# Recurrence emitted ahead of the other mixers, memory attention second with output tiles of its own, output projection from their tiles on

## The chip, the cores and the metric

One core of one Trainium2 chip runs the whole program, two transformer networks one behind the other. The metric is device microseconds of one execution, lower is better. Engine names are those of the profile: PE is TensorE (matmul), PEld its weight loads, DVE is VectorE, ACT ScalarE, POOL GpSimd, and SP the engine whose queue issues the large loads.

## The reference

Only the first network's front is touched, for 256 tokens of width 1024. Its three mixers read one normalised input `h`, and one projection joins them:

```python
h = rms_norm(x, attn_norm[l])
proj = h @ w_in[l]
q_da, k_da, v_da, rw_cols, q_mem = jnp.split(proj, [c1, c2, c3, c4], axis=-1)
o_da = diff_attention(q_da, k_da, v_da, positions, ...)        # 4 heads, 512 columns
o_rw = rwkv7_time_mix(rw_cols, ...)                            # 4 heads, 256 columns
mem_n = rms_norm(mem, mem_norm[l])
o_mem = memory_attention(q_mem, mem_n, w_mem_kv[l], ...)       # 4 heads, 256 columns
mixed = jnp.concatenate([o_da, o_rw, o_mem], axis=-1)
x = x + mixed @ w_out[l]
x = x + hierarchical_moe(rms_norm(x, ffn_norm[l]), ...)        # 16 experts
```

`diff_attention` takes two softmax maps per head and subtracts one from the other; `rwkv7_time_mix` is a recurrence over the tokens (state 64x64 per head). Everything behind the mixture of experts, four feed-forward layers and two more mixers, is the second network.

## The kernel before

The program is written as calls on tiles; a scheduler then sets each engine's order. It works through the emitted order and lets later work fill where it thinks that an engine would wait, so the emitted order is a priority. Once built, each engine's queue is fixed.

Weights come as 128x4096 fp32 tiles (2 MB) into a ring of three buffers named `raw` (`load`, L85 to L92; the issues are on SP). `split` (L94 to L101) makes of 1024 columns a rounded high part `wh` on ACT (L99) and the rest `wl` on DVE (L100), in a ring of three pairs here. Every projection takes three products per tile, high by high, low by high, high by low (`mm3`, L105 to L107, called "products" below); a projection of 512 columns over 1024 has 48 of them, in two PSUM banks.

`mixers` (L551 to L625) holds the change. The recurrence is a Python generator: `rwkv_inputs` (L644) projects its 1024 columns, and `rwkv` (L667) is emitted in pieces at each `next(rwkv)`. Between the pieces stand the attention's k projection (into `lent`), its q projection, the memory's transposes `memT` and key/value projection `mkv`, the head norms and transposes (`heads_T`), the memory's queries (`win_m`) and the v projection `dv`. Then come `diff_attn` (L1013), the last piece of the recurrence (its result is `Y`), `mem_attn` (L1064), the transposes of `Y` (L606), and the output projection.

- Vector stage of the recurrence: L698 to L746 make `kr`, `nb` and `kt` on DVE and ACT, with small PE steps at L705, L726, L750 and L758. The first products that need `nb` are at L777. L794 is the helper of the chain of 64x64 products behind it.
- Difference attention, per head and map: scores (L295, L296), added bias and row minimum on DVE (L301), exponential on ACT (L303), reciprocal (L309), scaling and subtraction (L1023 to L1026). Then transposes (L1033), the copy `pT` (L1035) and the products with `dv` (L1039 to L1041), which gather in two PSUM banks `po` until all four heads are done. At the end each half is copied (`do`, L1046), squared, summed (L1051), given its root on POOL (L112), scaled (L1053), transposed (L1056), scaled (L1058) and split into `oh` (L1061) and `ol` (L1062).
- Memory attention: scores L1076, minimum L1077, exponential L1080, scaling L1084, transposes L1095, copy L1098, products L1101.
- `project_back` (L345): eight k tiles of the mixed row (0 to 3 attention, 4 and 5 recurrence, 6 and 7 memory). It takes all but the last `tail` tiles for both token halves, then the tail half by half; half 0 gathers in two `acc` banks, half 1 in two `rk` banks.

PSUM has three `acc`, two `tr` and three `rk` banks. Behind the mixers, `logits` (L1108) and the routing at the head of `moe` (L1135) end in the first expert product, L1303. The experts' weights are loaded into buffers that fall free earlier: halves of 1 MB (L1267), the recurrence's scratch among them, `wh` and `wl` pairs (L1263) and `raw` tiles.

## Time and profile before

| what | us |
|---|---|
| median of 3 runs | 1427.64 (1427.21 to 1431.28) |
| the profiled execution's own time | 1430.63 |
| its span | 1428.9 |
| front: start of the trace to the end of the output projection | 188.0 |
| from there to the first expert product | 17.6 |

A trace row gives start, duration and, in brackets, the idle time before it with the instruction that ended it. PE's durations overlap, because matmuls are pipelined; the spacing of their starts tells what one costs. The fp32 score, transpose and small products may have several records per instruction. PEclk is the granted TensorE clock as a share of 2.4 GHz, so 0.50 is its level of 1.2 GHz. In the order listings below, names carry numbers that tell buffers apart, and the changed kernel's line numbers are higher (L105 to L107 are L117 to L119, lines further on 9 higher).

### The profile page before, as it was taken

The numbers are of one execution on the slowest core, as the hardware profiler recorded it, in microseconds if no ns is written. First come the engines' busy times: TensorE is split into PE (matmuls) and PEld (weight loads), VectorE is DVE, ScalarE is ACT, GpSimd is POOL, SyncE is SP. The second block draws the span as 40 slices with busy tenths as digits, with TensorE's granted clock in tenths as the row PEclk, the third lists the DMA queues.
The fourth block names the chain that finished last, engine by engine and source line by source line (L and its number), as shares of the span: only waits on it lengthen the run. The fifth ranks groups of instructions, "written<-read, shape, count | busy, mean of one in ns | idle before, by whom it ended". The sixth has DMA issues, their size and how long they took to land.

```text
span 1428.9 us, 18895 instructions
## 1 busy us (share of the span) xinstructions
PE 1378.0 (96%) x7650; PEld 1051.2 (74%) x7650; DVE 747.7 (52%) x1250; ACT 610.0 (43%) x961; POOL 77.5 (5%) x123
## 2 busy tenths in 40 slices
PE   8999989998998999999999999999999989999997
PEld 7787664343336888888777888878888877788886
DVE  6867641121116655457865655455554567555543
ACT  5545421011113544347454544345444366545442
POOL 1133100000000000000110000000000000000001
PEclk9999889999998999999999999999999999999999
DMA  7262489999956555446334555445553642464420
GB/s 315 93 230 91 185 327 414 409 424 428 422 216 236 183 191 184 153 171 251 115 106 147 184 191 183 178 178 188 189 205 125 241 158 75 139 229 177 177 89 30
DMA packets 35370, 293.81 MB, mean 206 GB/s; under 512 B 3728, under 2 KB 8112, under 8 KB 16080
## 3 DMA queue, kind: packets, MB, share of 16 engines
q1 hardware_dynamic: 29952, 286.58, 53.1%
q10 hardware_dynamic: 5328, 5.98, 1.3%
q8 instruction: 62, 1.02, 0.3%
q14 instruction: 28, 0.23, 0.0%
HBM read 291.45 MB, written 1.10 MB: 205 GB/s over the span
## 4 chain that ended last, share of the span: by engine, by line
PE 65%; DVE 3%; ACT 1%; issue 1%; ACTq 0%; POOLq 0%; POOL 0%
PE acc L105 20%; PE acc L107 20%; PE acc L106 20%; PE tr L213 1%; PE acc L329 1%; DVE wl L100 1%; PE tr L325 1%; PE acc L296 1%; PE acc L295 1%; PE acc L330 0%; ACT sq L119 0%; DVE h L376 0%; DVE h L378 0%; DVE xf L139 0%; ACT wh L99 0%
## 5 line engine op out<-in xcount | busy, mean ns | idle before, releaser
L100 DVE TENSOR_TENSOR wl<-raw,wh 128x1024 fp32r<-128x1024 f32 (+1 forms) x349 | 426.1, 1224 | 377.0 <-ACT wh L99 374.9
L99 ACT CAST wh<-raw 128x1024 fp32r<-128x1024 f32 (+1 forms) x349 | 364.6, 1048 | 408.6 <-PE acc L107 358.1
L105 PE MATMUL acc<-wh,xh 128*128 128x512 f32 (+1 forms) x896 | 334.5, 375 | 2.4 <-ACT xh L140 1.8
L107 PE MATMUL acc<-wh,xl 128*128 128x512 f32 (+2 forms) x896 | 333.2, 373 | 1.7 <-DVE xl L141 1.5
L106 PE MATMUL acc<-wl,xh 128*128 128x512 f32 (+1 forms) x896 | 333.1, 372 | 0.0
L105 PEld LDWEIGHTS acc<-wh,xh 128*128 128x128 f32 x896 | 170.4, 190 | 32.2 <-ACT xh L140 3.0
L107 PEld LDWEIGHTS acc<-wh,xl 128*128 128x128 f32 x896 | 170.3, 190 | 31.7 <-DVE xl L141 3.7
L106 PEld LDWEIGHTS acc<-wl,xh 128*128 128x128 f32 x896 | 170.5, 190 | 28.3 <-DVE lent L732 0.6
L107 PE MATMUL acc<-wh,hl 128*128 128x512 f32 x352 | 137.5, 391 | 0.0
L106 PE MATMUL acc<-wl,hh 128*128 128x512 f32 x352 | 137.1, 389 | 0.0
L105 PE MATMUL acc<-wh,hh 128*128 128x512 f32 x352 | 137.0, 389 | 0.0
L106 PEld LDWEIGHTS acc<-wl,hh 128*128 128x128 f32 x352 | 66.1, 188 | 13.8
L105 PEld LDWEIGHTS acc<-wh,hh 128*128 128x128 f32 x352 | 66.1, 188 | 13.5
L107 PEld LDWEIGHTS acc<-wh,hl 128*128 128x128 f32 x352 | 66.1, 188 | 13.4
L105 PE MATMUL acc<-xh,wh 128*128 128x256 f32 x224 | 67.6, 302 | 1.2 <-ACT wh L99 0.6
L106 PE MATMUL acc<-xl,wh 128*128 128x256 f32 x224 | 65.6, 293 | 0.6 <-DVE xl L141 0.6
L107 PE MATMUL acc<-xh,wl 128*128 128x256 f32 x224 | 65.7, 295 | 0.0
L111 POOL TENSOR_SCALAR rstd<-ss 128x1 f32<-128x1 f32 x22 | 9.3, 422 | 965.8 <-ACT sq L119 964.3
L1303 PE MATMUL acc<-half,xe 128*64 128x512 f32 x248 | 59.6, 596 | 0.0
L1336 DVE TENSOR_SCALAR yf<-tr,gate 128x512 f32<-128x512 f32 x16 | 12.0, 751 | 81.0 <-PE tr L1329 80.8
L105 PEld LDWEIGHTS acc<-xh,wh 128*128 128x128 f32 x224 | 45.2, 202 | 5.0 <-issue 2.4
L106 PEld LDWEIGHTS acc<-xl,wh 128*128 128x128 f32 x224 | 45.1, 201 | 1.1 <-DVE xl L141 0.9
(454 smaller groups left out, 1681.5 us busy)
## 6 DMA issues: line engine op xcount, KB each, us to landing
raw<-in_ffn SPq DMA_DIRECT2D x63, 2048.0 KB, 8.0
half<-in_moe SPq DMA_DIRECT2D x45, 1024.0 KB, 12.9
raw<-in_moe SPq DMA_DIRECT2D x13, 2048.0 KB, 16.0
raw<-in_hyb SPq DMA_DIRECT2D x7, 2048.0 KB, 8.2
wl<-in_moe SPq DMA_DIRECT2D x23, 512.0 KB, 13.4
wh<-in_moe SPq DMA_DIRECT2D x23, 512.0 KB, 14.4
raw<-in_win SPq DMA_DIRECT2D x4, 2048.0 KB, 10.7
raw<-in_swa SPq DMA_DIRECT2D x4, 2048.0 KB, 9.2
```

Of the source, the lines that this page charges most:

```text
L99: nc.scalar.copy(hi[:, :n], x)
L100: nc.vector.tensor_tensor(lo[:, :n], x, hi[:, :n].bitcast(F32), OP.subtract)
L105: mm(out, a[0], b[0], start=start, stop=False)
L106: mm(out, a[0], b[1], start=False, stop=False)
L107: mm(out, a[1], b[0], start=False, stop=stop)
L213: nc.tensor.transpose(ps[:, i * 128:(i + 1) * 128], m[:, i * 128:(i + 1) * 128], self.ident)
L295: nc.tensor.matmul(ps[:, 0:128], qT[r, 0:128], kT[r, 0:128], start=True, stop=True)
L296: nc.tensor.matmul(ps[:, 128:384], qT[r, 128:256], kT[r, :], start=True, stop=True)
L325: nc.tensor.transpose(pt[:, i * 128:(i + 1) * 128], s2[e][:, i * 128:(i + 1) * 128], self.ident)
L329: nc.tensor.matmul(po[r, :T], v[0][:, c:c + 64], pT[:, :T], start=True, stop=False)
L1303: last = mm(ps[c][e * 64:e * 64 + 64, :], xe[:, k, o + e * 64:o + e * 64 + 64], w[i][e][:, c * 512:c * 512 + 512], start=k == 0, stop=k == 7)
L1336: nc.vector.tensor_scalar(yf, po[a], gate[:, 0:1], None, OP.mult)
```

## The change

```diff
+class Joined:
+    def __init__(self, a, b):
+        self.a, self.b = a, b
+
+    def __getitem__(self, at):
+        p, k, t = at
+        n = self.a.shape[1]
+        return self.a[p, k, t] if k < n else self.b[p, k - n, t]
...
         parts = {}
-        for b, src in enumerate(wsrc):
-            wd = self.load(src)
-            for i in sorted(range(src.shape[-1] // 1024), key=lambda i: order.index(4 * b + i)):
-                parts[4 * b + i] = self.split(wd[:, i * 1024:(i + 1) * 1024])
+        raw = {}
+        for b in sorted(range(len(wsrc)), key=lambda b: order.index(4 * b)):
+            raw[b] = self.load(wsrc[b])
+            for k in [k for k in order if k not in parts]:
+                if k // 4 not in raw:
+                    break
+                parts[k] = self.split(raw[k // 4][:, k % 4 * 1024:(k % 4 + 1) * 1024])
...
-        rwkv = self.rwkv(self.rwkv_inputs(W, xh, xl, bc))
-        next(rwkv)
+        rw = self.rwkv_inputs(W, xh, xl, bc)
+        mem = [self.sb([D], "mem") for _ in range(2)]
+        for t in range(2):
+            nc.sync.dma_start(mem[t], self.I["mem"][t * 128:(t + 1) * 128])
+        Y = list(self.rwkv(rw))[-1]
         dist, nlam = self.diff_consts()
         k = project(W[3], 512, self.lent("wl"))
-        next(rwkv)
         self.bias_vectors()
-        q = project(W[2], 512, self.lent("wh"))
-        next(rwkv)
-        m = next(self.ring).tile([128, 4096], F32, name="mem", tag="raw")
-        mem = [m[:, :D], m[:, D:2 * D]]
-        for t in range(2):
-            nc.sync.dma_start(mem[t], self.I["mem"][t * 128:(t + 1) * 128])
         m = next(self.ring).tile([128, 4096], F32, name="memT", tag="raw")
...
         mkv = project(self.I["memkv"], 512, [self.sb([512], "mkv") for _ in range(2)], xm)
-        next(rwkv)
         kT = self.heads_T(k, 4, self.col("dak_g"), 1.0, "dkT")
-        qT = self.heads_T(q, 4, self.col("daq_g"), 0.125, "dqT")
-        next(rwkv)
         qm = project(self.I["win_m"], 256, [self.sb([256], "mq") for _ in range(2)])
         mqT = self.heads_T(qm, 2, self.col("memq_g"), 0.125, "mqT")
-        next(rwkv)
         mkT = self.heads_T([z[:, :256] for z in mkv], 2, self.col("memk_g"), 1.0, "mkT")
-        next(rwkv)
+        q = project(W[2], 512, self.lent("wh"))
+        om = [wk.tile([128, 2, T], F32R, name=self.nm("om"), tag=n, bufs=1) for n in ("mh", "ml")]
+        self.mem_attn(mqT, mkT, mkv, *om)
+        qT = self.heads_T(q, 4, self.col("daq_g"), 0.125, "dqT")
         v = project(W[4], 512, [self.sb([512], "dv") for _ in range(2)])
         oh, ol = (self.wk.tile([128, 8, T], F32R, name=self.nm("o"), tag=n, bufs=1) for n in ("xh", "xl"))
         self.diff_attn(qT, kT, v, dist, nlam, oh, ol)
-        Y = list(rwkv)[-1]
         scratch.close()
-        self.mem_attn(mqT, mkT, mkv, oh, ol)
...
+        oh, ol = (Joined(z[:, :6, :], m) for z, m in zip((oh, ol), om))
...
-            nc.scalar.copy(oh[:, 6 + j, :], po[:, :T])
-            nc.vector.tensor_sub(ol[:, 6 + j, :], po[:, :T], oh[:, 6 + j, :].bitcast(F32))
+            nc.scalar.copy(oh[:, j, :], po[:, :T])
+            nc.vector.tensor_sub(ol[:, j, :], po[:, :T], oh[:, j, :].bitcast(F32))
...
-MIX_ORDER = (0, 1, 2, 3, 6, 7, 4, 5)
-TAIL = {"mix": 2, 0: 5, "hyb": 5, 1: 4, 2: 2, "swa": 3, 3: 4}
+MIX_ORDER = (6, 7, 4, 5, 0, 1, 2, 3)
+TAIL = {"mix": 3, 0: 5, "hyb": 5, 1: 4, 2: 2, "swa": 3, 3: 4}
...
-           "a": ((8, 12), (128, 1), (260, 2), (384, 3), (512, 7), (1024, 2))}
+           "a": ((8, 12), (128, 1), (260, 2), (384, 3), (512, 9), (1024, 4))}
```

The whole recurrence now has the highest priority, and all else fills. `mem` lies in buffers of its own and is loaded early; memory attention follows its projections and writes `om`, which `Joined` shows to the output projection as tiles 6 and 7; the q projection comes later, and its weights take the ring buffer that `memT` leaves. Difference attention is last. The output projection loads the second half of its weights first and takes tiles 6, 7, 4, 5 ahead of 0 to 3, with a tail of three.

**First place: PE, the recurrence's vector stage.** In these rows acc_575 and acc_576 are the attention's k projection, tr_494 the transposes of the recurrence's norms. Before:

```order
L107 MATMUL acc_575<-wh_567,xl_97 128x512
L105 MATMUL acc_576<-wh_567,xh_96 128x512
L106 MATMUL acc_576<-wl_568,xh_96 128x512
L107 MATMUL acc_576<-wh_567,xl_97 128x512
L726 MATMUL tr_494<-ident,lent_457 128x128 x4
L105 MATMUL acc_575<-wh_571,xh_96 128x512
L105 MATMUL acc_576<-wh_571,xh_96 128x512
L229 MATMUL tr_840<-bias_const_838 32x384
```

Now (acc_1199 is the k projection, and its first product is the last row):

```order
L759 MATMUL rk_525<-c_94,boN_79_463 128x2 x3
L145 MATMUL tr_1268<-ident,mem_446 128x128 x4
L786 MATMUL rk_545<-kr_464,nb_465 64x128 x2
L786 MATMUL acc_633<-kr_464,kt_466 64x128 x2
L786 MATMUL acc_634<-kr_464,kt_466 64x128 x2
L786 MATMUL acc_633<-kr_464,kt_466 64x128 x2
L786 MATMUL rk_546<-kr_464,nb_465 64x128 x2
L786 MATMUL rk_545<-kr_464,nb_465 64x128 x2
L786 MATMUL rk_546<-kr_464,nb_465 64x128 x2
L814 MATMUL rk_567<-nb_465,kr_464 64x64 x4
L786 MATMUL acc_634<-kr_464,kt_466 64x128 x2
L117 MATMUL acc_1199<-wh_1183,xh_96 128x512
```

All 48 products of the k projection have moved from around and ahead of the vector stage's PE steps to behind the first products that need `nb`.

**Second place: PE, the third and fourth head of the difference attention.** dkT and dqT are its keys and queries, dv its values; NR, Z, S, DW and MT belong to the recurrence. Before:

```order
L903 MATMUL rk_1498<-DW_1438,MT_1437 64x64 x3
L295 MATMUL acc_1697<-dkT_1195,dqT_1222 128x128
L296 MATMUL acc_1697<-dkT_1195,dqT_1222 128x256
L1033 MATMUL tr_1724<-ident,sc_1662 128x128 x3
L903 MATMUL rk_1506<-S_1499,MT_1437 64x64 x4
L915 MATMUL rk_1779<-NR_627,Z_1393 64x64 x4
L915 MATMUL rk_1778<-NR_627,Z_1393 64x64 x4
L295 MATMUL acc_1708<-dkT_1195,dqT_1222 128x128
L296 MATMUL acc_1708<-dkT_1195,dqT_1222 128x256
L1039 MATMUL acc_1652<-dv_1514,pT_1728 128x128
L1040 MATMUL acc_1653<-dv_1514,pT_1728 128x128
```

Now:

```order
L1048 MATMUL acc_1844<-dv_1706,pT_1882 128x128
L1049 MATMUL acc_1845<-dv_1706,pT_1882 128x128
L1050 MATMUL acc_1845<-dv_1707,pT_1882 128x128
L307 MATMUL acc_1889<-dkT_1379,dqT_1679 128x128
L308 MATMUL acc_1889<-dkT_1379,dqT_1679 128x256
L1042 MATMUL tr_1916<-ident,sc_1854 128x128 x3
L307 MATMUL acc_1900<-dkT_1379,dqT_1679 128x128
L308 MATMUL acc_1900<-dkT_1379,dqT_1679 128x256
L1048 MATMUL acc_1844<-dv_1706,pT_1920 128x128
L1049 MATMUL acc_1845<-dv_1706,pT_1920 128x128
L1050 MATMUL acc_1845<-dv_1707,pT_1920 128x128
L117 MATMUL acc_1984<-wh_1990,om_1587 128x512
```

The recurrence's products between the heads are gone. What fills is 12 products of the memory's tiles at the first head's scores, and six at the fourth, of which the last row is the first.

**Third place: PE, the end of the difference attention.** Rows with o are the output projection's, tr_1751 and tr_1943 the transposes of `do`, acc_1890 and its like memory scores. Before:

```order
L1040 MATMUL acc_1653<-dv_1514,pT_1737 128x128
L1041 MATMUL acc_1653<-dv_1515,pT_1737 128x128
L1076 MATMUL acc_1890<-mkT_1414,mqT_1362 128x256 x2
L1076 MATMUL acc_1902<-mkT_1414,mqT_1362 128x256 x2
L1056 MATMUL tr_1751<-ident,do_1742 128x128 x4
L1076 MATMUL acc_1914<-mkT_1414,mqT_1362 128x256 x2
L1056 MATMUL tr_1769<-ident,do_1760 128x128 x4
L1095 MATMUL tr_1927<-ident,ms_1879 128x128 x4
L105 MATMUL rk_1983<-wh_1987,o_1586 128x512
```

Now:

```order
L1050 MATMUL acc_1845<-dv_1707,pT_1929 128x128
L117 MATMUL acc_1985<-wh_1990,om_1587 128x512
L118 MATMUL acc_1985<-wl_1991,om_1587 128x512
L119 MATMUL acc_1985<-wh_1990,om_1588 128x512
L117 MATMUL acc_1985<-wh_1994,om_1587 128x512
L118 MATMUL acc_1985<-wl_1995,om_1587 128x512
L119 MATMUL acc_1985<-wh_1994,om_1588 128x512
L1065 MATMUL tr_1943<-ident,do_1934 128x128 x4
L1065 MATMUL tr_1961<-ident,do_1952 128x128 x4
L614 MATMUL tr_1971<-ident,Y 128x128 x2
L614 MATMUL tr_1976<-ident,Y 128x128 x2
L117 MATMUL acc_1984<-wh_1998,o_1778 128x512
```

The memory's scores have left this place for six products; the transposes of the recurrence's `Y`, and with them the 24 products of tiles 4 and 5, stand behind the transposes of `do`.

## Rows read from the trace of the kernel before

**Rows 1.** The page: its head.

```profile
span 1428.9 us, 18895 instructions
```

**Rows 2.** Windows of the front: each engine's busy us and instructions, granted clock, DMA.

```profile
17.62:39.85 22.23, 22.23 (x187) 21.73 (x185) 14.30 (x22) 15.23 (x26) 1.08 (x8) 1.00 0.66 271
39.85:54.97 15.12, 15.12 (x77) 11.90 (x76) 14.60 (x32) 10.41 (x20) 5.17 (x7) 1.00 0.02 4
54.97:119.14 64.17, 63.06 (x742) 51.86 (x741) 44.80 (x77) 26.26 (x42) 20.18 (x20) 1.00 0.54 199
119.14:147.35 28.21, 27.82 (x437) 22.00 (x436) 21.32 (x90) 17.75 (x60) 6.33 (x7) 1.00 0.11 37
147.35:158.01 10.66, 7.28 (x25) 4.79 (x25) 10.36 (x26) 6.49 (x20) 4.96 (x8) 0.66 0.09 12
158.01:187.99 29.98, 29.98 (x130) 22.40 (x131) 11.58 (x22) 9.69 (x18) 1.46 (x1) 0.95 0.86 351
187.99:205.63 17.64, 13.11 (x76) 12.59 (x74) 12.87 (x45) 5.32 (x10) 1.88 (x4) 0.61 0.86 350
```

**Rows 3.** Timeline of SP, and a window of the start of the experts.

```profile
209.32 0.33 SPq L91 DMA_DIRECT2D raw<-in_moe  x1
...
205.00:210.00 5.00, 5.00 (x24) 1.99 (x23) 0.69 (x1) 0.05 (x1) 0.00 (x0) 0.96 0.01 3
```

**Rows 4.** Timeline of DVE at both ends of the vector stage, and the splits between.

```profile
39.68 0.42 DVE L657 TENSOR_TENSOR cur<-acc,bc 128x256 f32<-128x256 f32 x1 [0.30 <-PE acc L107]
...
54.78 0.40 DVE L738 TENSOR_TENSOR nb<-lent,iw 128x256 f32<-128x256 f32 x1
...
L100 DVE TENSOR_TENSOR wl<-raw,wh 128x1024 fp32r<-128x1024 f32 x5 | 6.1, 1215 | 0.0
```

**Rows 5.** Timeline of PE: two products of the k projection.

```profile
47.68 0.39 PE L106 MATMUL acc<-wl,xh 128*128 128x512 f32 x1
47.91 0.39 PE L107 MATMUL acc<-wh,xl 128*128 128x512 f32 x1
```

**Rows 6.** Timeline of PE: scores of one map, transposes of one head, the start behind.

```profile
137.24 0.49 PE L295 MATMUL acc<-dkT,dqT 64*128 64x128 f32 x2
...
138.09 0.82 PE L1033 MATMUL tr<-ident,sc 128*128 128x128 f32 x3
138.87 0.46 PE L903 MATMUL rk<-S,MT 64*64 64x64 f32 x4
```

**Rows 7.** Timeline of DVE: first and last operations of the fourth head.

```profile
138.92 0.28 DVE L301 CUSTOM_DVE_ANT_0 sc<-acc,dbias 128x128 f32<-128x128 f32 x1
...
143.10 0.74 DVE L1026 SCALAR_TENSOR_TENSOR sc<-sc,den,sc 128x128 f32<-128x128 f32 x2
```

**Rows 8.** Groups of ACT instructions, 119 to 162 us: count, busy us, mean ns, idle.

```profile
L420 ACT ACTIVATE dv<-acc,rstd 128x512 f32<-128x512 f32 x2 | 1.2, 674 | 0.0
L99 ACT CAST wh<-raw 128x1024 fp32r<-128x1024 f32 x1 | 1.0, 1045 | 1.0 <-PE acc L107 1.0
```

**Rows 9.** Timeline of PE behind the attention's last product, which ends at 147.35.

```profile
147.58 2.26 PE L1076 MATMUL acc<-mkT,mqT 64*128 64x256 f32 x8 [0.23 <-ACT do L1046]
152.25 1.12 PE L1056 MATMUL tr<-ident,do 128*128 128x128 f32 x4 [2.41 <-DVE do L1053]
158.01 0.80 PE L105 MATMUL rk<-wh,o 128*128 128x512 f32 x1 [0.74 <-ACT o L1061]
```

**Rows 10.** Windows of 5 us around that wait.

```profile
150.00:155.00 5.00, 2.75 (x8) 1.88 (x8) 4.77 (x13) 2.04 (x8) 3.15 (x5) 0.57 0.01 2
155.00:160.00 5.00, 4.26 (x14) 3.07 (x14) 5.00 (x14) 3.71 (x11) 0.00 (x0) 0.50 0.47 133
160.00:165.00 5.00, 5.00 (x25) 3.60 (x24) 0.80 (x4) 0.58 (x1) 0.00 (x0) 0.90 1.02 429
```

**Rows 11.** Transfers by line, median us from issue to landing.

```profile
raw<-in_memkv SPq DMA_DIRECT2D x1, 2048.0 KB, 7.6
```

## The prediction

> **What bounds the kernel now.** I read the page's head first, for the span of the profiled execution [rows 1], then windows over the front, where each column says how busy an engine is [rows 2]. The reader is to see there that PE is the full engine: 22.23 of 22.23 us, then 15.12 of 15.12, 63.06 of 64.17 and 27.82 of 28.21, the last with DVE at 21.32 and ACT at 17.75 beside it. The recurrence's small products, the projections and the difference attention are interleaved so that something is nearly always ready. Only one place is open: behind the attention's last product, 147.35 to 158.01, PE shows 7.28 of 10.66 and the granted clock is 0.66 of 2.4 GHz.
>
> Second, what follows the front. The experts' buffers are full before the routing is known: between 205 and 210 the DMA engines are at 0.01, and SP issues the next expert load only at 209.32, when a first buffer falls free [rows 3]. No transfer waits to be pulled ahead, so I count a delay of the front as a delay of the end, one for one.
>
> So the question is how much PE time the new order leaves idle between 17.6 us and the first expert product, and how much of the one hole it closes. PE's work is the same in both; the sum below is over idle time and time at half clock.
>
> **A, the recurrence's vector stage.** Between the last input product (39.85) and the first product with `nb`, DVE works from 39.68 until `nb` is written at 54.78 + 0.40 = 55.18 [rows 4], 15.5 us. Five splits lie in it, 1.215 us each, 6.1 in all [rows 4]. PE filled these 15.12 us with the 48 products of the k projection, whose starts are 0.23 apart [rows 5]: 11.0 us, leaving 4.1 for the stage's own small steps. In the new order all 48 stand behind the first products that need `nb`, and an engine's queue is fixed, so they can't fill. The stage itself gets shorter: one split is left ahead of `nb`, so 15.5 - 4 x 1.2 = 10.7, and `nb` comes at 50.4. PE then has 4.1 us to do in 10.5: 6.4 idle. Lower bound 4, if the stage also loses most of the rows that ACT shares with the splits' high parts; upper 10, if the splits only lay in DVE's waits and the stage stays near 15. The splits' rows have no idle time before them, so I stay near the first: **+6**.
>
> **B, the difference attention by itself.** It used to run among the recurrence's last products. Now the recurrence is done, and only 18 memory-tile products are left to lie beside it, 12 at the first head and six at the fourth. Ahead of its first minimum stand two copies `dv` of 0.67 and one cast `wh` of 1.05 on ACT [rows 8], and one split of 1.22 on DVE [rows 4]: 3.6 in all. The chain of one head runs through DVE and ACT; the fourth head took from 138.92 to 143.10 + 0.74 = 143.84 [rows 7], 4.92 us, with six recurrence operations among them. Without them it can lose at best what DVE has idle or elsewhere in it; scaled by DVE's busy share (21.32 of 28.21 [rows 2]) that is 3.7. At half clock its two score pairs cost about 0.6 more, so 5.5 is the upper end. I take 4.5, nearer to the measured head, since most of those operations stood beside a wait. 3.6 + 4 x 4.5 + 1.6 for the last transposes and products gives 23.2. PE's work in it: per head two maps of scores at 0.85 (137.24 to 138.09), the transposes 0.78 (138.09 to 138.87) [rows 6] and about as much, 0.87, for the products with `dv`: 3.35, four times 13.4; and 18 products at 0.23 are 4.1. 23.2 - 17.5 = **+6**, between 2.5 (heads of 3.7) and 10 (heads of 5.5).
>
> The Trainium skill, "Perfetto Trace Analysis", section "Optimization Strategy", says that a kernel with several regimes may gain by interleaving them. The window with PE at 27.82 of 28.21 beside a DVE at 21.32 [rows 2] is such an interleaving, and the change separates what it holds; by that advice B is a loss, by a count of busy time alone it would be nothing. No number above depends on it.
>
> **C, the end of the difference attention.** Before, 10.66 us passed from the last product to the first of the output projection. What PE did in it is worth less: 12 memory scores at 2.26 / 8 = 0.28 each, 3.4, and 12 transposes that took 1.12 for four at half clock [rows 9], so about 1.7 at full, 5.1 together. Lost: 5.6, and some 1.5 more since the first 3 us of products also ran at half clock (0.50 in 155 to 160, 0.90 in 160 to 165 [rows 10]), 7.1 in all. Now the scores are gone from here and six products, 1.4, stand in their place; the transposes of `Y`, with the 24 products of tiles 4 and 5, stand behind the transposes of `do` in PE's queue, so the recurrence's tiles do not cover the wait although they are ready. Two splits of 1.2 stand in DVE's queue in the tail's chain; the memory's minima and the recurrence's last normalisation have left it. I set those against each other, with about 1 us in favour of the shorter queue: 10.66 - 1 - 3.1 + 1.5 = 8.1, so **+1** (from -2, if the chain falls to about 7, to +4, if both splits delay it in full and the clock is half for 24 products).
>
> **D, the second load of the q weights.** The q projection's weights now wait for the ring buffer that `memT` leaves, freed by the last `mkv` product. Its first product comes some 9 us behind that in PE's order, by my count of the products between; a 2 MB load of this kind takes 7.6 us [rows 11], with a split of about 2 us to the first product. **+1** (0 to 3). SP holds nothing behind it that the front needs sooner; the experts' loads there go into buffers that were full in time anyway [rows 3].
>
> **E, the clock behind the stall of A.** The one stall of before was followed by some 3 us of products at half clock, 1.5 lost [rows 10]; A's stall is shorter and has small steps in it: **+1** (0 to 4).
>
> **F, small waits and re-ordered pieces.** The 1.5 us of PE idle between 54.97 and 147.35 (1.11 and 0.39 [rows 2]) may partly go, since now everything fills behind the recurrence: **-1** (-3 to +2). The copies into `om` are those that went into the shared tile before, and `Joined` only chooses between tiles while the program is built: nothing. `mem` now loads early on, beside the first weights (DMA at 0.66 until 39.85 [rows 2]); hidden, since it is needed only behind the whole vector stage, and if it held up the input weights by its size, 1 MB of 2 MB loads of 7.6 us [rows 11], that would be under 4, which the range holds.
>
> **Sum.** 6 + 6 + 1 + 1 + 1 - 1 = +14. It is made against the profiled execution's 1430.63 (span 1428.9 [rows 1]), which stands 3.0 above the median 1427.64; against the median it gives 1427.6 + 14 = **1441.6**.
>
> **The rivals.**
>
> *Contention, not order, set the pace (not slower), 0.13.* Then the engines, once the recurrence has left, run the attention at heads of 3.7: B is 2.5, C falls to -1.5, A stands at its lower bound 4, D and E are nothing, F is -2: +3, 1431, no change that can be measured; with A at nothing as well (the stage short enough to be covered by its own steps) it is slightly faster, 1427 to 1424. For it: DVE's 14.60 busy of 15.12 in the vector stage and 10.36 of 10.66 in the tail [rows 2], so chains there were queues. Against: DVE does 8.5 us of its own between the splits, twice PE's 4.1, so A can't vanish without a faster DVE. It decides if heads come at or below 4.1 us.
>
> *The clock stays at half through the whole attention, 0.17.* PE would do 17.5 us of work in 23, in pieces, behind a stall; half clock (1.2 GHz) there makes heads 5.5 and B 10, E 5, C +4, A, D and F as above: 6 + 10 + 4 + 1 + 5 - 1 = +25, 1453. For it: a window with PE at 2.75 of 5 was granted 0.57, and the next, with 4.26 of 5, still 0.50 [rows 10]. Against: with PE at 27.82 of 28.21 the clock was 1.00, and so far it rose again within 3 us of products. The Trainium skill, "TensorE: Matmul & The Clock Gate", section "HAM oscillation — how this bites in real kernels", puts the cost of being throttled again after waits at half of the throttled time; by it the roughly 10 us at half clock behind the tail of before would have cost 5, while by the rows only the products in them, 1.5, count as lost, since the rest was a wait on DVE and ACT. The trace so far bears the smaller number out, and no run yet shows which holds in the attention.
>
> *The delay is not passed on, or the tiles do cover the tail, 0.06.* If the experts' loads absorbed the shift, or if PE could start on tiles 4 and 5 while the attention ends (24 products, 5.5 us), the total would be 1427 down to 1422. Against the first: full buffers and a DMA share of 0.01 as the experts start [rows 3]. Against the second: the order of the queue, third place above.
>
> **How the numbers follow.** The forecast has 0.64, the rivals 0.13, 0.17 and 0.06. About 0.3% (4.3 us) is what a measurement can tell from no change. Slower than that: the forecast's 0.64, all of the clock rival, less 0.01 for the low ends of the terms falling together, 0.80. Within it: 0.13, most of the first rival, a part of the third and that 0.01. Faster: 0.07, from the first's and third's low ends. The range runs from the first rival's +3 at 1430 to 1455, a little over the clock rival's 1453; below lies about 0.12, above about 0.08.
>
> **What would show it.** PE idle for some 6 us between 40 and 51, where 15.12 of 15.12 stood. PE at about three quarters in the 23 us of the difference attention. A tail of about 10 us between the last product with `dv` and the first of tiles 4 and 5. The output projection ending near 202 where 188.0 stood, the first expert product near 220, and the same distance from there to the end. The forecast is wrong in A if `nb` comes before 46 or k products stand ahead of it; in B if heads come at 4 us or 5.5; and as a whole if the distance from the first expert product to the end changes by more than 3 us.

## The result, and the profile after

| | before | after |
|---|---|---|
| median, us | 1427.43 (1426.86 to 1431.28, 4 runs) | 1445.2 (1443.2 to 1446.9, 4 runs) |
| ratio | | 1.0118, 95% interval 1.0099 to 1.0137 |
| span of the profiled execution | 1428.9 | 1443.0 |
| end of the output projection | 188.0 | 203.9 |
| first expert product | 205.6 | 221.8 |
| from there to the end | 1223.3 | 1221.2 |

Slower, by 17.8 us between the medians and by 14.1 between the two profiled executions; the forecast was +14, 1441.6. That the 14.1 lands on the 14 is closer than a single pair of executions can carry. The delay is complete at the first expert product (+16.1) and nearly all of it reaches the end. Over all the profiled executions below, the stretch behind the first expert product took 1217.5 to 1223.9 us, with no relation to the front; so the time of the first expert product is the finer yardstick for an edit of the front, and each experiment is given with it.

Windows of the kernel after, cut at its own milestones (the answer to [rows 2]; columns as there):

```profile
17.62:39.97 22.35, 22.35 (x181) 21.38 (x179) 14.67 (x23) 15.35 (x26) 2.24 (x11) 1.00 0.66 266
39.97:54.47 14.50, 11.05 (x76) 8.26 (x75) 13.21 (x32) 6.29 (x15) 2.35 (x3) 0.67 0.01 4
54.47:151.25 96.78, 95.77 (x1164) 78.00 (x1162) 62.74 (x129) 44.27 (x90) 28.85 (x30) 1.00 0.37 134
151.25:176.93 25.68, 21.93 (x86) 15.03 (x85) 14.49 (x64) 11.55 (x40) 0.00 (x0) 0.73 0.58 238
176.93:186.83 9.90, 4.62 (x19) 3.25 (x19) 6.75 (x9) 5.05 (x9) 3.71 (x4) 0.72 0.57 205
186.83:203.92 17.09, 17.09 (x74) 14.05 (x73) 6.32 (x9) 3.81 (x5) 0.91 (x1) 0.96 0.91 350
203.92:221.77 17.85, 12.85 (x76) 12.12 (x75) 13.04 (x46) 5.33 (x10) 1.89 (x4) 0.63 0.51 198
```

The rows are: input products; the recurrence's vector stage up to the first product of the k projection; everything up to the end of the v projection; the difference attention up to its last product with `dv`; its tail up to the first output product of tiles 4 and 5; the other output products; routing. The second, fourth and fifth are the three places of the forecast, and each has idle PE time and a granted clock of 0.67 to 0.73. The long row between them is dense (1.01 idle) at full clock, and routing is as long as before (17.64).

What PE waited for between 17 and 222 us (total, times, longest):

```profile
PE tr L1065 <- DVE do L1062: 4.6, 2, 2.9
PE tr L735 <- DVE lent L731: 3.4, 1, 3.4
...
PE tr L1042 <- DVE sc L1035: 2.2, 1, 2.2
PE acc L1048 <- ACT pT L1044: 1.5, 2, 0.9
```

L1065 is the tail, L735 the vector stage, L1042 and L1048 the first and last heads. These are 11.7 us; the same list of before holds 2.4 + 0.7 for its tail. Over the whole stretch from 17.62 to the first expert product PE is idle for 18.5 us where 9.4 stood, and busy for 185.7 where 178.6 stood, with the same products to do. So 9.1 of the 16.1 are waits and 7.1 are longer busy time; I put the latter down to the clock, which was at half for 30.7 us up to the end of the output projection where 10.2 stood. The timeline of PE in the vector stage, and two heads of the attention:

```profile
44.47 0.77 PE L735 MATMUL tr<-ident,lent 128*128 128x128 f32 x4 [3.45 <-DVE lent L731]
...
52.07 0.48 PE L786 MATMUL rk<-kr,nb 64*64 64x128 f32 x2
...
54.47 0.76 PE L117 MATMUL acc<-wh,xh 128*128 128x512 f32 x1
...
163.19 0.90 PE L1042 MATMUL tr<-ident,sc 128*128 128x128 f32 x3
...
168.75 0.90 PE L1042 MATMUL tr<-ident,sc 128*128 128x128 f32 x3
```

The clock was at half from 44.83 to 55.07 and from 160.88 to 174.53. In the second stretch PE has no idle time: two heads come 5.56 apart because PE itself is slow, the upper end that the forecast gave for a head.

### The profile page after: what moved, and what is told of

The parts are those of the page before. It is cut to its first block, busy times and chain, and to the rows that moved or that the text cites. A ratio compares the mean times of both kernels' runs of the same rounds, so it can differ in the third digit from the quotient of the medians.

```text
span 1443.0 us, 18906 instructions
## 1 busy us (share of the span) xinstructions
PE 1381.3 (96%) x7650; PEld 1053.0 (73%) x7650; DVE 749.2 (52%) x1250; ACT 611.5 (42%) x961; POOL 77.4 (5%) x123
## 4 chain that ended last, share of the span: by engine, by line
PE 64%; DVE 3%; ACT 1%; issue 1%; ACTq 0%; POOLq 0%; POOL 0%
PE acc L117 20%; PE acc L119 20%; PE acc L118 19%; PE tr L225 1%; PE acc L341 1%; DVE wl L112 1%; PE tr L337 1%; PE acc L308 1%; PE acc L307 1%; PE acc L342 0%; ACT sq L131 0%; DVE h L391 0%; DVE h L393 0%; DVE xf L151 0%; ACT wh L111 0%
## 5 line engine op out<-in xcount | busy, mean ns | idle before, releaser
L118 PEld LDWEIGHTS acc<-wl,hh 128*128 128x128 f32 x352 | 66.1, 188 | 13.6
L315 ACT ACTIVATE sc<-sc,nm 128x128 f32<-128x128 f32 x80 | 35.6, 447 | 27.3 <-DVE nm L313 27.3
```

Of the source, the lines that this page charges most:

```text
L118: mm(out, a[0], b[1], start=False, stop=False)
L315: nc.scalar.activation(s[:, sl], s[:, sl], AF.Exp, bias=nm[:, b:b + 1], scale=-1.0, accum_out=den[:, b:b + 1])
```

## Experiments

All kernels were compared with the kernel before on the same chip; "first" is the first expert product in the profiled execution (205.6 before, 221.8 after).

**The products taken from the vector stage put back.** The edit, on the changed kernel:

```diff
-        Y = list(self.rwkv(rw))[-1]
+        rwkv = self.rwkv(rw)
+        next(rwkv)
         dist, nlam = self.diff_consts()
         k = project(W[3], 512, self.lent("wl"))
+        Y = list(rwkv)[-1]
```

> The changed kernel with one thing put back: the 48 products of the k projection stand again beside the recurrence's vector stage; difference attention still runs last and alone. Theory (the new order opens holes on PE; the first is this one: 3.5 us idle and 10 us at half clock): the stage is filled again, PE at 1.00 clock there, and the whole program comes back by about 7 us, to 1438 (1436 to 1441). Rival (a conserved hole: PE lacks these products later, where the recurrence's small products then have nothing beside them, so the idle time only moves): 1445 within 2 us.

Measured: 1447.98, ratio 1.0135 (1.0115 to 1.0155), first at 226.1. My theory fell, and the loss is even above the rival's 1443 to 1447. The stage is full (15.00 of 15.00 busy, clock 1.00), and the time did not come back; new waits stand behind it:

```profile
40.00:55.00 15.00, 15.00 (x76) 11.98 (x76) 11.99 (x28) 6.60 (x15) 2.35 (x3) 1.00 0.21 74
55.00:119.00 64.00, 61.33 (x809) 50.65 (x809) 40.92 (x76) 28.79 (x51) 15.37 (x18) 0.95 0.41 150
119.00:135.00 16.00, 12.15 (x166) 9.23 (x165) 9.63 (x20) 7.87 (x27) 4.84 (x4) 0.89 0.09 31
```

2.67 us idle in the second row and 3.85 in the third are together more than the 3.45 that were filled. I read the second row so that the k projection's products, used up at 40 to 55, were missing beside the recurrence's small ones. The third row's waits are those of the memory attention for its own chain (2.9 us for the copy `mpT`, 1.0 for `ms`). The scheduler also made another order of the whole front (the recurrence's last products come at 154.6, against 138.0 in the changed kernel), so how much of the loss is the one and how much the other stays open.

**One half of the change at a time.** The recurrence emitted whole in front, all else as before:

```diff
-        rwkv = self.rwkv(self.rwkv_inputs(W, xh, xl, bc))
-        next(rwkv)
+        Y = list(self.rwkv(self.rwkv_inputs(W, xh, xl, bc)))[-1]
...
-        Y = list(rwkv)[-1]
```

> The kernel before with one thing changed: the recurrence is emitted whole in front of all else; memory attention, its tiles and the output projection as before. Theory (the recurrence in front costs about 7 us in the vector stage and about as much in an attention by itself): 1441 (1437 to 1447). Rival (the loss comes from the memory attention's new place and the output order): 1432 or less.

Measured: 1448.29, ratio 1.0135 (1.0112 to 1.0158), first at 226.3: as slow as the theory said and 1.3 us above its range. Then the other half, with the recurrence in pieces and everything else as in the change (the pieces stand behind k, ahead of `memT`, behind `mkv`, behind the head transposes of k, behind `mqT` and ahead of q; the rest behind the difference attention):

```diff
-        Y = list(self.rwkv(rw))[-1]
+        rwkv = self.rwkv(rw)
+        next(rwkv)
...
         self.diff_attn(qT, kT, v, dist, nlam, oh, ol)
+        Y = list(rwkv)[-1]
```

> The changed kernel with the recurrence emitted in pieces between the others, as before; memory attention second with tiles of its own and the output projection's new order stay. Theory (what costs is the recurrence in front, through the vector stage and the attention by itself): the loss goes, 1427 (1422 to 1431). Rival (the memory attention's place, the later q projection and the new order of the projection's tiles cost as much): 1436 or more.

Measured: 1446.68, ratio 1.0127 (1.0104 to 1.0151), first at 224.8, the rival's number. Each half alone costs as much as both together, so the costs do not add: "the recurrence in front" is enough by itself, and it is not needed. What the three slow kernels share is that the difference attention runs behind the recurrence's last products instead of among them: its last product with `dv` starts at 176.7 in the change, 168.7 and 180.2 in the halves, against 147.1 before. That this place alone makes the loss is not shown. In the second half PE is also idle for 6.8 us between 55 and 163, ahead of the attention, where the kernel before has 1.5 between 54.97 and 147.35. In the first half the attention's window (first row) shows the clock rival at its purest:

```profile
151.26:168.99 17.73, 17.11 (x53) 11.78 (x53) 10.71 (x47) 6.92 (x26) 1.26 (x2) 0.50 0.66 260
169.00:182.00 13.00, 11.67 (x36) 7.47 (x36) 9.95 (x24) 7.84 (x23) 2.53 (x4) 0.50 0.13 51
```

PE is shown busy for 17.11 of 17.73 us and was granted half the clock throughout; the clock was back only at 182.0, 30.7 us after it fell. Of this kernel's 20.6 us at the first expert product, 5.4 are more idle time and 15.2 longer busy time.

**The q projection back in its place**, on the second half:

```diff
         self.bias_vectors()
+        q = project(W[2], 512, self.lent("wh"))
...
         next(rwkv)
-        q = project(W[2], 512, self.lent("wh"))
```

> The run with the recurrence emitted in pieces (memory attention second, tiles of its own, new output order), and with the q projection back ahead of the memory's, its weights loaded early as before. Theory L (the late q projection and its late weights left PE without work around 60 and 124 us, and pushed the difference attention behind the recurrence): 1432 or less. Rival P (the place of the memory attention does it: whatever is emitted ahead takes PE's open places beside the recurrence, so the difference attention still comes last, with nothing beside it): 1438 or more.

Measured: 1442.42, ratio 1.0090 (1.0068 to 1.0113), first at 218.8. About 6 us come back, and the kernel is still 13 us from the one before: rival P's number. The waits near 61 and 128 shrink, as theory L has it, but others appear between 70 and 160: PE's idle time falls by 1.0 us only, its busy time by 5.0, with less half clock. The attention's products run at 160.3 to 173.7, behind the recurrence's last (154.9), although it is emitted ahead of its last piece. Rival P's reason is only part of the 13, though: PE is idle for 7.3 us in the attention and its tail, where the kernel before has 3.4 in the tail, and for 8.2 us ahead of them, from 55 to 160, where it has 1.5 up to the tail.

**Work added where PE waits.** Products whose result nobody reads, on the changed kernel; first 24 around the attention's first scores:

```diff
         self.diff_attn(qT, kT, v, dist, nlam, oh, ol)
+        ps = self.rkb()
+        for i in range(24):
+            nc.tensor.matmul(ps, om[0][:, 0, :128], om[0].rearrange("p a t -> p (a t)"), start=True, stop=True)
```

> The changed kernel with 24 products added that nobody reads, 16 around the difference attention's first scores and 8 in the wait behind them, 5.5 us at full clock where 3.7 are idle. Theory (PE at half clock sets the heads: 5.6 us from head to head, PE without idle time): the clock stays at 1.00, the heads come at about 4.5 us, and the added work costs nothing: 1445 or less. Rival (the heads' chain over DVE and ACT sets them at any clock): heads as before, and 2 to 4 us more, 1447 or more.

Measured: 1442.53, ratio 1.0102 (1.0081 to 1.0123), first at 222.7. 5.5 us of work cost 0.9 us at the first expert product and nothing in the program's time; 0.7 of the 0.9 already stood at the end of the v projection (151.96 against 151.25), ahead of the added work. The stretch from the first to the last product with `dv`, here and (second fence) in the changed kernel:

```profile
164.69:177.77 13.08, 10.67 (x53) 7.78 (x52) 6.19 (x31) 5.46 (x20) 0.00 (x0) 0.87 0.17 71
```

```profile
160.42:176.93 16.51, 15.88 (x55) 11.23 (x55) 8.07 (x37) 6.14 (x22) 0.00 (x0) 0.59 0.35 146
```

Three heads behind the first, six output products among them in both (in the first, one head's transposes, 0.55, already stand ahead): 13.6 / 3 = 4.5 per head at 0.87, 16.51 / 3 = 5.5 at 0.59. With the clock mostly full (not at 1.00 throughout, as the theory had it) PE waits again for the minimum on DVE (two waits of 0.75), so a head is about 4.5 by its chain and 5.5 by PE's clock: both theories hold, each at its clock. The run with q back in its place has the same three heads and six products at 0.88, with nothing added, and they take 4.6 each:

```profile
160.28:174.00 13.72, 11.73 (x55) 8.19 (x55) 9.21 (x42) 5.84 (x21) 1.44 (x2) 0.88 0.64 251
```

The first two rows differ by 2.9 us (16.51 less 13.6) and by 10.24 us of half clock (13.65 in the changed kernel, 3.41 here). The Trainium skill, "TensorE: Matmul & The Clock Gate", section "HAM oscillation — how this bites in real kernels", counts half of the throttled time as lost; an estimate by it for these 10.24 us is 5.1. The rows show the smaller number: at the higher clock PE waits for the chain instead.

In the vector stage, 15 such products behind the first piece of the recurrence:

```diff
-        Y = list(self.rwkv(rw))[-1]
+        rwkv = self.rwkv(rw)
+        next(rwkv)
+        ps = self.acc()
+        for i in range(15):
+            nc.tensor.matmul(ps, xh[:, 0, :128], xh[:, 0:2, :].rearrange("p a t -> p (a t)"), start=True, stop=True)
+        Y = list(rwkv)[-1]
```

> The changed kernel with 15 products added that nobody reads, in the 3.5 us hole of the recurrence's vector stage. Theory (the hole's cost is more than its idle time, through the half clock of the 10 us behind it): the granted clock stays at 1.00 there and the program gets shorter with more work in it, 1442 (1440 to 1444). Rival (DVE's chain sets the stage, the clock costs nothing in it): 1445 within 1 us.

Measured: 1450.58, ratio 1.0155 (1.0134 to 1.0177), first at 227.2: neither number came out. In the stage itself it did what was expected: the clock stayed at 1.00 and the first product with `nb` started at 50.62 instead of 52.07 (the first row shows PE alone):

```profile
40.00:55.00 15.00, 14.26 (x107) 1.00 0.01 4
```

```profile
50.62 0.45 PE L791 MATMUL rk<-kr,nb 64*64 64x128 f32 x8
```

But the scheduler planned the rest otherwise, as in the first experiment (recurrence's last products at 155.8), so the program's time says nothing on the hole. With `range(6)` in the same edit PE's order stays that of the change:

> The changed kernel with six products added that nobody reads, 1.4 us in the 3.5 us hole of the vector stage; every other instruction of PE stands in the order of the changed kernel, which was not so with 15. Theory (the hole also costs through the clock behind it): less half clock in 45 to 55, the first products with nb about 1 us earlier, and the first expert product as much earlier. Rival (other work stands open there, and what is won in the stage is lost at the next wait): the first expert product within 0.5 us of 221.8.

Measured: 1443.65, ratio 1.0113 (1.0095 to 1.0131), first at 221.9. The stage's row and the first product with `nb`:

```profile
40.00:55.00 15.00, 11.90 (x81) 9.25 (x82) 13.77 (x34) 5.80 (x14) 2.50 (x4) 0.77 0.01 4
```

```profile
51.60 0.48 PE L791 MATMUL rk<-kr,nb 64*64 64x128 f32 x2
```

The half clock lasted 6.83 us instead of 10.24, `nb`'s products came 0.47 earlier and the attention's first scores 0.78 earlier (151.77 against 152.55). The first expert product did not: half clock in the attention's tail lasted 10.24 us here, against 6.83. Such differences also come without an edit at the place: in the run with 24 products the vector stage has the changed kernel's order, and its half clock lasted 13.65 us. Too small an effect to settle the stage's share; the rival's number came out.

**The attention's end.** On the changed kernel, the transposes of `Y` ahead of the difference attention, and output sums in one `acc` and three `rk` banks:

```diff
+        for t in range(2):
+            ps = self.trp()
...
         self.diff_attn(qT, kT, v, dist, nlam, oh, ol)
         scratch.close()
-        for t in range(2):
-            ps = self.trp()
...
-                               tags=("acc", "acc", "rk", "rk")))
+                               tags=("acc", "rk", "rk", "rk")))
```

> The changed kernel with the transposes of Y written ahead of the difference attention, and three of the four output sums in rk banks instead of two, so that about 36 products of the memory's and the recurrence's tiles may run inside the attention and at its end. Theory (the attention by itself leaves PE idle and so at half clock; products are there to fill it): idle time in the attention and its tail falls from about 9 us to under 4, the clock stays at 1.00 for most of it, 1438 (1434 to 1441). Rival (the heads' chain over DVE and ACT and the tail's chain set the pace, and products put between only delay them): 1443 or more.

Measured: 1441.36, ratio 1.0093 (1.0072 to 1.0114), first at 218.6, 3.2 earlier. The direction of the theory, 0.4 above its range and below the rival's 1443: idle time from the v projection's end to the tail's end fell only from 9.0 to 7.7 us. The heads are fuller; in the tail, where the products were wanted most, PE still waits:

```profile
151.31:180.95 29.64, 26.79 (x121) 18.88 (x119) 19.68 (x70) 16.42 (x46) 0.00 (x0) 0.88 0.68 269
180.95:187.96 7.01, 2.17 (x8) 1.43 (x8) 3.51 (x6) 2.52 (x5) 3.02 (x4) 0.54 0.07 28
```

The scheduler had used up the products before the tail began. The same idea on the kernel before, where the tail is the one hole: difference attention in two parts, the transposes of `Y` between them, tiles 4 and 5 first:

```diff
-        self.diff_attn(qT, kT, v, dist, nlam, oh, ol)
+        da = self.diff_attn(qT, kT, v, dist, nlam, oh, ol)
+        next(da)
         Y = list(rwkv)[-1]
+        for t in range(2):
+            ps = self.trp()
...
+        list(da)
         scratch.close()
...
         self.staggered(4, first, second)
+        yield
...
-MIX_ORDER = (0, 1, 2, 3, 6, 7, 4, 5)
+MIX_ORDER = (4, 5, 0, 1, 2, 3, 6, 7)
```

(with the changed kernel's loads by `MIX_ORDER` and the three `rk` banks).

> The kernel before, with only its one hole worked on: the end of the difference attention is emitted behind the transposes of Y, the output projection takes the recurrence's tiles 4 and 5 first (then 0 to 3, 6, 7) and has three rk banks. Six products stand ahead of the transposes of do and some 12 behind them. Theory (what counts is what PE has beside the attention's last chain): the wait of 2.4 us ahead of the transposes of do goes, with part of the half clock behind it: 1424 (1421 to 1426). Rival (the chain over DVE, ACT and POOL ends as late, and the products moved there only come off a dense stretch that then ends at the same time, or the extra copies of Y stand in that chain): 1427 or more.

Measured over ten runs: 1426.74, ratio 0.9985 (0.9974 to 0.9996), first at 202.8, 2.8 earlier (2.1 at the end of the output projection; the other 0.7 came in the routing, which was not edited). Between theory and rival, and the one version that is faster than both kernels, by 0.15% (0.04 to 0.26). Its tail, timeline of PE:

```profile
151.63 0.69 PE L608 MATMUL tr<-ident,Y 128*128 128x128 f32 x2 [1.81 <-DVE Y L966]
...
154.44 0.79 PE L105 MATMUL rk<-wh,o 128*128 128x512 f32 x1
...
157.50 0.60 PE L1062 MATMUL tr<-ident,do 128*128 128x128 f32 x4
```

The first output product came at 154.44 instead of 158.01 [rows 9]; the wait is now for `Y` and 1.81 long, where 2.41 stood, and the half clock lasted 6.83 us instead of 10.24. `do` is transposed later than before (157.50 against 152.25), since its transposes now queue behind those of `Y`; that this takes part of the gain back is likely and was not tested. PE's idle time up to the first expert product is the same in both kernels (9.4 us), so the gain is in its busy time, which is 2.8 us shorter with less half clock.

**Something else last.** If the attention alone at the end is the cost, then difference attention second and the memory last should cure it, with the memory's 48 products to lie beside it. On the kernel above, whose lines for the memory are taken out further up, first with the recurrence whole in front, then in pieces:

```diff
         Y = list(rwkv)[-1]
-        for t in range(2):
-            ps = self.trp()
...
         list(da)
+        for t in range(2):
+            ps = self.trp()
...
+        mkv = project(self.I["memkv"], 512, [self.sb([512], "mkv") for _ in range(2)], xm)
+        mkT = self.heads_T([z[:, :256] for z in mkv], 2, self.col("memk_g"), 1.0, "mkT")
         scratch.close()
```

> The kernel before with the whole recurrence emitted in front, as in the change, but difference attention second and the memory's key and value projection and attention last; its tail behind the transposes of Y, output tiles 4, 5 first, three rk banks. The attention's heads then stand beside the recurrence's last products in PE's order, and the memory's 48 products behind its tail. Theory P (what costs is the difference attention by itself at the end, not the recurrence in front): the end is filled, 1431 or less, with at most the vector stage's hole left. Rival (the recurrence in front costs by itself, through the vector stage and the late projections): 1438 or more.

> The same with the recurrence in pieces between the others, as before: difference attention inside the recurrence, the memory's projection and attention last, and the output products of tiles 4, 5 and 0 to 3 beside the memory attention. Theory P: no place of the front is left in which PE has only one chain, 1421 (1417 to 1425), faster than both kernels. Rival (the memory's 48 products are missed earlier, beside the recurrence's small products, and the hole moves there): 1427 or more.

Measured: 1472.61, ratio 1.0313 (1.0293 to 1.0333), first at 249.3; and 1463.32, ratio 1.0242 (1.0224 to 1.0261), first at 240.5. The theory's numbers were missed by far; the rivals' are met, but for a reason that neither had. PE's longest waits of the second, and SP's timeline:

```profile
PE acc L105 <- ACT wh L99: 16.1, 1, 16.1
PE tr L599 <- DVE Y L966: 6.4, 2, 5.7
```

```profile
145.52 2.49 SPq L1273 DMA_DIRECT2D half<-in_moe  x5
148.06 0.48 SPq L91 DMA_DIRECT2D raw<-in_memkv  x1
```

The memory's weights stand in SP's queue behind five expert halves, which wait for the recurrence's scratch to fall free at 145.5; they land 17 us after their issue, behind those halves. The first had the same wait, 8.4 us. The front's first part did what was expected in the second: last product with `dv` at 129.6, before the recurrence's last at 137.3. So this was mended (`memkv` and the first output weights loaded early by hand, the memory's rows in tiles of their own, the memory's projection ahead of the transposes of `Y`):

```diff
         v = project(W[4], 512, [self.sb([512], "dv") for _ in range(2)])
+        mem = [self.sb([D], "mem") for _ in range(2)]
+        for t in range(2):
+            nc.sync.dma_start(mem[t], self.I["mem"][t * 128:(t + 1) * 128])
+        mraw = self.load(self.I["memkv"])
...
+        self.pre = {0: self.load(self.I["wout"][0])}
...
-MIX_ORDER = (4, 5, 0, 1, 2, 3, 6, 7)
+MIX_ORDER = (0, 1, 2, 3, 4, 5, 6, 7)
```

> The run with difference attention second and the memory last, recurrence in pieces, mended where its trace showed the wait: the memory's weights are issued behind those of v, so ahead of the five expert halves in SP's queue; the memory's rows get tiles of their own; the first output weights are issued early as well; the memory's projection is emitted ahead of the transposes of Y, and the output projection takes its tiles in the order 0 to 7. Theory P (difference attention inside the recurrence, and at the end only chains that have products beside them): the 16.1 us wait for the memory's weights and the 5.7 us wait for Y go, the first expert product comes at 198 to 204 where it stood at 205.6 in the kernel before, and the program takes 1422 (1418 to 1428). Rival (the memory's late projection is missed earlier, or its chain over POOL and ACT at the end is as long as the attention's): first expert product later than 208, 1430 or more.

Measured: 1435.53, ratio 1.0043 (1.0026 to 1.0060), first at 212.2. 28 us better than unmended, and still slower than the kernel before: the rival's number. Windows from the attention's last scores on:

```profile
119.80:133.80 14.00, 10.17 (x166) 8.32 (x167) 6.54 (x19) 6.93 (x20) 7.99 (x8) 0.96 0.13 40
133.80:159.10 25.30, 24.88 (x217) 20.61 (x217) 19.92 (x43) 11.53 (x20) 5.12 (x6) 0.95 0.38 135
159.10:182.00 22.90, 18.84 (x63) 11.38 (x63) 9.62 (x23) 9.54 (x25) 1.76 (x3) 0.70 0.62 264
182.00:196.00 14.00, 14.00 (x66) 11.44 (x64) 6.68 (x9) 3.11 (x4) 0.64 (x1) 1.00 0.98 396
```

The difference attention's tail (first row) still waits 3.8 us, now in the middle; and in the third row the memory attention lies by itself, 4.1 idle and 0.70 of the clock. PE's busy time up to the first expert product is that of the kernel before (178.7 and 178.6), so the whole loss of 6.5 us is idle time. In these orders whichever attention was last had such a row. In the kernel before memory attention is last too, but it lies beside the tail and the output products of other tiles, where PE is busy for 29.98 of 29.98 us [rows 2]. I read it so that what stands beside the last chain counts, not which chain it is.

## Why the prediction was right

The sum was right (+14 forecast, +14.1 between profiled executions, +17.8 between medians, inside the range), and so was its ground: PE dense before, three places in the new order where it is not, and the delay passed on. Its terms were less good than their sum: A's surplus and E's shortfall cancel, and C, D and the tail of the program give back part of what B lacks, which is luck. The terms follow, against the profile after, and ahead of them the two rows of DVE that A rests on:

```profile
49.01 0.40 DVE L747 TENSOR_TENSOR nb<-lent,iw 128x256 f32<-128x256 f32 x1
...
50.61 0.40 DVE L747 TENSOR_TENSOR nb<-lent,iw 128x256 f32<-128x256 f32 x1
```

- **A and E, the vector stage: +6 and +1.** `nb` was forecast for 50.4; its two halves were begun at 49.01 and 50.61, and PE's first product with it started at 52.07. One split lay in the stage, as counted. But the idle time was 3.45, not 6.4, and the clock was at half for 10.24 us, not the few of the forecast: A was sized too large and E too small, because PE's small steps, slowed down, fill the wait for DVE (8.65 us busy up to `nb`'s product where 4.1 were counted). Together: 3.45 idle and, of 9.6 us at half clock, between the 1.45 that the full clock gave back in the run with 15 products and half of it, 4.8: 5 to 8. That a hole here is a loss that could be taken back alone was not shown: three runs tried (k products, 15 and six spare ones) and none had an earlier first expert product.
- **B, the attention by itself: +6.** 25.68 us from the v projection's end to the last product with `dv`, 23.2 forecast, for the same 17.5 of work: 8.2. The head of 4.5 was right for a clock near full (4.5 at 0.87 and 4.6 at 0.88 in two runs); in the changed kernel it was 5.5, which the forecast itself had named as the sign of being wrong in B. So B was mis-sized by the clock, and the clock rival came true for two heads and fell short of its +25, because the clock rose again behind 13.65 us.
- **C, the tail: +1.** 9.90 us from the last product to the first of tiles 4 and 5 (9.66 were forecast), less 3.1 of work in it, plus 0.7 for the products at half clock until 188.2: 7.5 lost against 7.1 before, so +0.4. The recurrence's tiles did stand ready and did not cover it.
- **D, the q weights: +1.** Nothing: no wait for them is in PE's list. Of the forecast's terms only this one named a cost that was not there.
- **F: -1.** 1.01 idle from 54.47 to 151.25, where 1.5 stood: -0.5.

Added up: 5 to 8, 8.2, 0.4, 0 and -0.5 give 13 to 16, against 16.1 at the first expert product. *Passed on:* 1221.2 from there to the end against 1223.3, so the third rival is out. *Contention as the pace:* heads of 4.5 at 0.87 of the clock are above its 4.1, and it is out too.

What the forecast did not see is which part of the change is to blame. It wrote A to the recurrence in front and B to the late attention, as if each could be undone. The runs show something else for B: either half of the change is enough to put the difference attention behind the recurrence, where its chain has too little beside it. How much of a half's cost that place makes, and how much the new waits ahead of it, stays open, and so does A's share; no edit of the changed kernel brought more than 3.2 us back at the first expert product.

## What to carry to other kernels

Where one engine is full because several chains lie beside each other, count for a new order not the work but which chain will be last and what stands beside it: a chain over DVE, ACT and POOL of some 25 us, alone, costs its idle PE time and then the clock. Products that fill one wait may be missing at another; before you credit a filled hole, ask what filled the next one. And before moving a load late in a program's order, look at what its queue holds ahead of it that waits for a buffer.

## What the hardware showed that was not expected

- More work made it no slower: 24 products nobody reads, 5.5 us at full clock, moved the first expert product by 0.9 us, 0.7 of it from ahead of them, and left the program's time as it was (ratio 1.0102 against 1.0118, overlapping intervals).
- A PE that the profile shows busy can be granted half the clock: 17.11 of 17.73 us busy at 0.50 with the recurrence alone in front. Busy time of small products is no sign of a full clock; the clock column has to be read beside it.
- A queue held by a buffer: one load behind five that waited for scratch came with a wait of 16.1 us on PE, the largest single one of all runs; issued ahead of them, it left no such wait.
